# Three ada modulations as TensorE sums, rows spread by step-zero weights, two ga blocks ahead of gb, conv taps back on VectorE

## The chip, the core and the metric

One NeuronCore of a Trainium2 chip. The metric is the device time of one execution in microseconds (us); the kernel before takes 895.0 us (median of three runs, 894.83 to 895.03). Engines are named as in the profile: PE (TensorE), DVE (VectorE), ACT (ScalarE), POOL (GpSimd), SP (the queue that issues all DMAs).

## What is computed

One layer of a diffusion backbone: 512 latent tokens and 256 context tokens of width 1024, all in fp32.

```
mods(6 x 1024) = silu(c) @ w_ada + b_ada          # sh1 sc1 gt1 sh2 sc2 gt2; the same for c_ctx
hl = rmsnorm(x)*(1+sc1)+sh1 ; hc likewise
v, g, xr, gt, ga, gb = split(hl @ w_in)           # xr also of hc
y_a = silu(layernorm(dwconv31(v*sigmoid(g)))) @ w_proj_conv
rec = rglru scans, forward and backward, of dwconv4(xr), started from the context's last state
y_b = (rec * gelu(gt)) @ w_proj_lru
y   = (sigmoid(ga)*y_a + sigmoid(gb)*y_b) @ w_out
x   = x + gt1 * rmsnorm(y)
z   = dwconv3x3((rmsnorm(x)*(1+sc2)+sh2) @ w_up)
x   = x + gt2 * rmsnorm((silu(z_g) * z_v) @ w_down)
```

The six modulations are vectors of 1024. Here m counts them: m = 0, 1 are sh1, sc1 (made early on PE, not touched), m = 2 is gt1, m = 3 is sh2, m = 4 is sc2, m = 5 is gt2.

## The kernel before, in words

Features lie on partitions, tokens in columns. Each fp32 operand of a large product is split into a high part (rounded, on ACT) and a low part (the rest), and `mm3` makes three products, high x high, high x low, low x high. A `block` is eight slices of 128 input features with three products each: 24 products of 512 columns for one block of 128 output features. Weights arrive in the order that the calls of `queue` write down: SP loads a raw tile (three buffers), ACT makes the high part (L122), POOL the low part (L123), or DVE for entries with `eng=V`; `W(key, look)` converts up to `look` entries ahead and asks for DMAs two further. The schedule is manual: each engine runs its instructions in the order of the code, and waits are put in by what tiles an instruction reads and writes.

The order of the work: a start, in which the input is normalised and the first products are made; the LRU loop (L656, rounds b = 1 to 8), in which each round makes xr(b), v(b+1), g(b+2) and the four gate products of b-1 (`gate_mm`), whose results stay in PSUM tiles of 1024 columns (two halves of 512; a gate uses columns 0 to 767); then gt, gb and yb blocks, with ga blocks behind them; the LayerNorm of the conv branch (mean, variance, rstd); the ya blocks; the output projection (y_ps); and the FFN, which takes the last 390 us.

Modulations m = 2 to 5 are summed on DVE: `ada_step(k, w, acc)` multiplies a tile of 128 x 1024 weights with a scalar per partition and adds it to `ggb`, eight steps for a modulation. For m = 2 the steps stand among the context work of the start, for m = 3 two in each of rounds 2 to 5, for m = 4 in the LayerNorm stage, for m = 5 in halves in the FFN. `ada_cols` then sums over partitions by four PE products with ones (four column blocks of 256), copies the result and turns it into columns by two transposes; for m = 2 and 3 that is in rounds 2 and 6. `ada_rows` makes, for m = 2 and 5, a row vector on all partitions: DVE scales the identity by each of eight columns (`dg`), and PE multiplies ones with that, 512 columns at a time (L333). The LayerNorm's rstd row is made the same way (L837, L839).

The depthwise conv of width 31 is a chain of single taps on DVE, handed out by `fill(n)`: n taps at this place in DVE's order. Channel blocks go in pairs. For the last pair (6, 7) the 12 highest taps are not DVE's: `offload(n)` has ACT make the products (L536) and POOL add them (L538), and the pair starts on DVE when all 24 are issued:

```
while n_glu[0] < b0 + 2 or b0 == 6 and off["k"] < 2 * n_off:
    yield False
```

`decay_rates` computes the LRU's decay constants by a chain of small POOL instructions behind one DVE reciprocal (L387). The g2 block's low part is POOL's and stands behind that chain.

Lines to follow: L123 low parts; L303 and L301 `ada_step`; L308, L315 `ada_cols`; L327, L333 `ada_rows`; L512, L504 conv taps; L536, L538 offloaded taps; L554 to L567 the conv of xr; L588 gate tanh; L603 `e` (`r_dve`); L607 `u` (`i_dve`); L809 mean; L830 variance; L839 rstd.

Of the kernel before, what the change touches and what calls it, by code (L numbers as in the profile page):

```python
# [37 lines left out]
def backbone_kernel(es: ExitStack, tc: tile.TileContext, x, ctxt, par, wadq, wada, win, wgate, wpc, wpl, wout,  # L38
# [145 lines left out]
    queue(("g", 2), win[10], wb)  # L184
# [20 lines left out]
    for b in range(NB):  # L205
        queue(("ga", b), win[32 + b], wb)
# [91 lines left out]
    def ada_step(k, w, acc):  # L298
        s = sT[:, k, 0:1]
        if k == 0:  # L300
            V.tensor_scalar(out=acc, in0=w, scalar1=s, scalar2=None, op0=ALU.mult)  # L301
        else:
            V.scalar_tensor_tensor(out=acc, in0=w, scalar=s, in1=acc, op0=ALU.mult, op1=ALU.add)  # L303

    def ada_cols(m, acc, big=None):
        big = cv_tile("ada_cp") if big is None else big
        for j in range(4):
            PE.matmul(big[32 * j:32 * j + 32, 0:256], ones[:, 0:32], acc[:, 256 * j:256 * j + 256], start=True, stop=True)  # L308
        R = t_tile("R2")
        V.tensor_copy(R[:, 0:256], big[:, 0:256])  # L310

        def rest():
# [8 lines left out]

    def ada_rows(m, gain, dst, big=None):
        cl = adl[:, 8 * m:8 * m + 8]
        V.tensor_mul(cl, cl, col(gain))
        dg = [t_tile("dg") for _ in range(2)]
        for n in range(8):
            V.tensor_scalar(out=dg[n // 4][:, 128 * (n % 4):128 * (n % 4) + 128], in0=idn, scalar1=cl[:, n:n + 1],  # L327
                            scalar2=None, op0=ALU.mult)
# [120 lines left out]
    def ctx_h(g, p, i):  # L449
# [19 lines left out]
    ctx_h(0, 0, 3)  # L469
    ctx_h(0, 1, 4)  # L470
# [4 lines left out]
    ctx_h(1, 0, 5)  # L475
    ctx_h(1, 1, 6)
# [50 lines left out]
    n_off = 12  # L527
# [128 lines left out]
    for b in range(1, NB + 1):  # L656
# [31 lines left out]
        fill(0 if last else 2 if b in (2, 6) else 4)  # L688
# [71 lines left out]
    turn[0] = 1  # L760
# [28 lines left out]

# [446 lines left out]
```

## Time and profile before

| | |
|---|---|
| median of 3 runs | 895.0 us (894.83 to 895.03) |
| the profiled execution | 892.42 us, span 890.6 us |
| PE busy | 848.2 us (95%), 4114 products |
| PE weight loads | 686.2 us (77%) |
| DVE busy | 689.3 us (77%), 952 instructions |
| ACT busy | 444.9 us (50%) |
| POOL busy | 441.3 us (50%) |
| chain that ended last | PE 70%, DVE 18%, ACT 5%, issue 4% |

Busy time of PE includes the overlap of pipelined products, so a stage with 100% may still hold a few spare tenths, and a stage below 100% has real gaps. The gaps are found in a timeline: a bracket at a line's end gives the idle time ahead of it and what ended it. PEclk is the clock granted to PE, as a share of full speed.

### The profile page before, as it was taken

The numbers are of one execution on the slowest core, as the hardware profiler recorded it, in microseconds if no ns is written. First come the engines' busy times: TensorE is split into PE (matmuls) and PEld (weight loads), VectorE is DVE, ScalarE is ACT, GpSimd is POOL, SyncE is SP. The second block draws the span as 40 slices with busy tenths as digits, with TensorE's granted clock in tenths as the row PEclk, the third lists the DMA queues.
The fourth block names the chain that finished last, engine by engine and source line by source line (L and its number), as shares of the span: only waits on it lengthen the run. The fifth ranks groups of instructions, "written<-read, shape, count | busy, mean of one in ns | idle before, by whom it ended". The sixth has DMA issues, their size and how long they took to land.

```text
span 890.6 us, 11044 instructions
## 1 busy us (share of the span) xinstructions
PE 848.2 (95%) x4114; PEld 686.2 (77%) x4114; DVE 689.3 (77%) x952; ACT 444.9 (50%) x634; POOL 441.3 (50%) x248
## 2 busy tenths in 40 slices
PE   7997999999999799999897999999999999999997
PEld 6776877877887688887675889988888888888775
DVE  4384799997997999596887345799999898998314
ACT  5282776776667834324833346535434344344322
POOL 1246454554546498946333222446545555547810
PEclk9998999999999999999998999999999999999999
DMA  9943133332123033223534411214333333333502
GB/s 356 384 165 107 60 118 130 107 114 76 60 77 105 33 118 96 95 94 142 193 132 149 166 43 52 93 63 141 118 109 117 118 106 119 107 118 118 166 1 95
DMA packets 31397, 105.98 MB, mean 119 GB/s; under 512 B 3440, under 2 KB 3568, under 8 KB 31344
## 3 DMA queue, kind: packets, MB, share of 16 engines
q1 hardware_dynamic: 31344, 105.29, 34.4%
q8 instruction: 32, 0.52, 0.2%
q14 instruction: 21, 0.17, 0.1%
HBM read 103.17 MB, written 2.10 MB: 118 GB/s over the span
## 4 chain that ended last, share of the span: by engine, by line
PE 70%; DVE 18%; ACT 5%; issue 4%; POOL 2%; DMA 1%; DVEq 0%; SPq 0%; POOLq 0%; ACTq 0%
PE up_ps L135 8%; PE up_ps L136 8%; PE up_ps L134 8%; DVE cv L512 4%; PE xr_ps L134 2%; PE xr_ps L135 2%; PE xr_ps L136 2%; DVE rec L626 2%; DVE ggb L303 2%; PE y_ps L135 2%; PE y_ps L134 2%; PE y_ps L136 2%; PE yb_ps L136 1%; PE yb_ps L135 1%; PE yb_ps L134 1%
## 5 line engine op out<-in xcount | busy, mean ns | idle before, releaser
L123 POOL TENSOR_TENSOR wlo<-raw,whi 128x1024 fp32r<-128x1024 f32 x118 | 293.3, 2498 | 204.2 <-ACT whi L122 203.8
L1034 DVE SCALAR_TENSOR_TENSOR cv<-zall,P,cv 128x512 f32<-128x512 f32 x240 | 161.9, 744 | 0.2
L512 DVE SCALAR_TENSOR_TENSOR cv<-glu,P,cv 128x512 f32<-128x512 f32 x208 | 140.4, 744 | 0.0
L122 ACT ACTIVATE whi<-raw 128x1024 fp32r<-128x1024 f32 x121 | 125.5, 1051 | 21.0 <-issue 8.0
L134 PE MATMUL up_ps<-Ahi,whi 128*128 128x512 f32 (+1 forms) x352 | 131.8, 375 | 0.0
L136 PE MATMUL up_ps<-Ahi,wlo 128*128 128x512 f32 (+1 forms) x352 | 131.7, 374 | 0.0
L135 PE MATMUL up_ps<-Alo,whi 128*128 128x512 f32 (+1 forms) x352 | 131.6, 374 | 0.0
L135 PEld LDWEIGHTS up_ps<-Alo,whi 128*128 128x128 f32 x352 | 66.0, 188 | 13.3
L136 PEld LDWEIGHTS up_ps<-Ahi,wlo 128*128 128x128 f32 x352 | 66.0, 188 | 13.2
L134 PEld LDWEIGHTS up_ps<-Ahi,whi 128*128 128x128 f32 x352 | 66.0, 188 | 13.1
L1020 POOL TENSOR_TENSOR acl<-fo,ach 128x512 fp32r<-128x512 f32 x20 | 26.0, 1301 | 85.5 <-ACT ach L1017 85.5
L1034 DVE SCALAR_TENSOR_TENSOR cv<-zall,P,cc 128x512 f32<-128x512 f32 x40 | 43.2, 1109 | 21.2 <-ACT cc L1008 21.2
L1006 ACT ACTIVATE zall<-up_ps 128x512 f32<-128x512 f32 x40 | 23.8, 594 | 63.5 <-PE up_ps L136 63.5
L588 ACT ACTIVATE gate_ps<-gate_ps,P 128x768 f32<-128x768 f32 x32 | 28.0, 875 | 36.2 <-PE gate_ps L136 35.7
L1017 ACT ACTIVATE ach<-fo 128x512 fp32r<-128x512 f32 x20 | 12.7, 633 | 66.9 <-DVE fo L1016 66.9
L303 DVE SCALAR_TENSOR_TENSOR ggb<-wa,sT,ggb 128x1024 f32<-128x1024 f32 (+1 forms) x35 | 40.1, 1146 | 0.4
L134 PE MATMUL xr_ps<-Ahi,whi 128*128 128x512 f32 x56 | 23.2, 414 | 8.8 <-DVE e L603 8.8
L538 POOL TENSOR_TENSOR off_acc<-off_acc,off_prod 128x512 f32<-128x512 f32 x22 | 28.5, 1318 | 3.9 <-ACT off_prod L536 3.9
L136 PE MATMUL g_ps<-Ahi,wlo 128*128 128x512 f32 x56 | 23.1, 412 | 5.8 <-POOL wlo L123 5.7
L134 PE MATMUL yb_ps<-rgh,whi 128*128 128x512 f32 x64 | 25.8, 404 | 2.5 <-ACT whi L122 2.5
L1008 ACT ACTIVATE cc<-up_ps,P 128x512 f32<-128x512 f32 x40 | 27.3, 682 | 1.9 <-DVE cv L1034 1.9
L136 PE MATMUL yb_ps<-rgh,wlo 128*128 128x512 f32 x64 | 26.0, 406 | 2.2 <-POOL wlo L123 2.2
(386 smaller groups left out, 2156.1 us busy)
## 6 DMA issues: line engine op xcount, KB each, us to landing
raw<-in_win_dram SPq DMA_DIRECT2D x48, 512.0 KB, 3.4
raw<-in_wup_dram SPq DMA_DIRECT2D x40, 512.0 KB, 3.4
wa<-in_wada_dram SPq DMA_DIRECT2D x24, 512.0 KB, 5.6
raw<-in_wdn_dram SPq DMA_DIRECT2D x22, 512.0 KB, 3.4
wa<-in_wadq_dram SPq DMA_DIRECT2D x16, 512.0 KB, 9.2
raw<-in_wpl_dram SPq DMA_DIRECT2D x8, 512.0 KB, 3.3
raw<-in_wpc_dram SPq DMA_DIRECT2D x8, 512.0 KB, 3.6
raw<-in_wout_dram SPq DMA_DIRECT2D x8, 512.0 KB, 3.4
```

Source lines behind the costliest of these rows:

```text
L122: S.activation(out=flat(hl[0]), in_=flat(t), func=AF.Copy)
L123: eng.tensor_sub(flat(hl[1]), flat(t), flat(hl[0]))
L134: PE.matmul(o, lh, rh, start=first, stop=False)
L135: PE.matmul(o, lh, rl, start=False, stop=False)
L136: PE.matmul(o, ll, rh, start=False, stop=last)
L303: V.scalar_tensor_tensor(out=acc, in0=w, scalar=s, in1=acc, op0=ALU.mult, op1=ALU.add)
L512: V.scalar_tensor_tensor(out=cv[b] if k else glu[:, b, 0:T], in0=glu[:, b, k:k + T], scalar=col("dw31", 31 * b + k, 1), in1=cv[b], op0=ALU ...
L538: G.tensor_add(a, a, o)
L588: S.activation(out=lru[b, d, q], in_=lru[b, d, q], func=AF.Tanh, scale=0.5, bias=hb[:, i:i + 1])
L1008: S.activation(out=c, in_=ps.rearrange("p (r c) -> p r c", c=GW), func=AF.Copy, scale=col("dw9", 9 * (i + FW * (1 - s)) + 4, 1))
L1020: G.tensor_sub(acl[:, i, :], fo[i, 0], ach[:, i, :])
L1034: V.scalar_tensor_tensor(out=o, in0=zz[i, s][:, k // 3:k // 3 + GH, k % 3:k % 3 + GW], scalar=col("dw9", 9 * (i + FW * (1 - s)) + k, 1), i ...
```

## The change

- The sums of m = 2, 3 and 4 go to PE. `ada_pe` multiplies `sT[:, k, :]` (32 columns, the first of which is silu(c)) with four column blocks of 256 of the weight tile, and adds up over k in PSUM. m = 2: all eight k at once after the context's xr product. m = 3: two k after the last gate product of rounds 2 to 5, into the free columns 768 to 1023 of that gate's PSUM tile, from which DVE copies or adds them to `ggb`; the turning into columns goes to the end of round 6. m = 4: four k ahead of the variance product, four ahead of ya(0).
- In the loop three taps stand where two steps stood, and rounds 2 and 6 have four taps in place of two at the detour's place.
- `ada_rows` and the LayerNorm's rstd have no diagonal any more: `spread` multiplies, for each of the columns, a weight operand that repeats that column 128 times (step zero) with the identity. The m = 2 rows are issued after ya(3) and no more after ya(5).
- `decay_rates` is issued ahead of the last quarter of hl (`ada_h(3)`); g2's low part goes to DVE.
- ga(0) and ga(1) stand ahead of gb(0) in the queue and in the code.
- The last conv pair has 2 taps on ACT and POOL in place of 12; the first yb round takes 20 taps in place of 8.

```diff
-    queue(("g", 2), win[10], wb)
+    queue(("g", 2), win[10], wb, eng=V)
...
+    for b in (0, 1):
+        queue(("ga", b), win[32 + b], wb)
     queue(("gb", 0), win[40], wb)
...
+    def ada_pe(ks, ws, o, first, last):
+        for n, (k, w) in enumerate(zip(ks, ws)):
+            for j in range(4):
+                PE.matmul(o[32 * j:32 * j + 32, :], sT[:, k, :], w[:, 256 * j:256 * j + 256],
+                          start=first and n == 0, stop=last and n == len(ws) - 1)
...
+    def spread(o, cols, n):
+        for i in range(n):
+            PE.matmul(o[:, 128 * i:128 * i + 128], cols[:, i:i + 1].broadcast_to([128, 128]), idn, start=True, stop=True)
...
     ctx_t(0, 0)
+    decay_rates()
     ada_h(3)
-    for k in range(3):
-        ada_step(k, wa[k], ggb)
-    decay_rates()
...
     block(psA[:, T:T + TP], ready[0], chi, clo)
+    big = cv_tile("ada_cp")
+    ada_pe(range(NB), wa, big[:, 0:256], True, True)
...
+    rest = ada_cols(2, big[:, 0:256], big)
+    w = W(("g", 2), 2, 2)
+    block(psg, w, Ahi, Alo, range(2))
+    rest()
+    block(psg, w, Ahi, Alo, range(2, NB))
...
-    n_off = 12
+    n_off = 2
...
-        if 2 <= b <= 5:
-            for k in (2 * b - 4, 2 * b - 3):
-                ada_step(k, was[k], ggb)
-        else:
-            fill(3)
+        fill(3)
         r_dve(b - 1, 1)
         fill(3)
-        gate_mm(b - 1, 1, 1)
+        ps = gate_mm(b - 1, 1, 1)
+        if 2 <= b <= 5:
+            o = ps[:, TA:1024]
+            ada_pe((2 * b - 4, 2 * b - 3), (was[2 * b - 4], was[2 * b - 3]), o, True, True)
+            if b == 2:
+                V.tensor_copy(ggb[:, 0:256], o)
+            else:
+                V.tensor_add(ggb[:, 0:256], ggb[:, 0:256], o)
+        if b == 6:
+            ada_cols(3, ggb[:, 0:256])(ps[:, T:1024])
         gate_tanh(b - 1, 1, 1)
...
+    turn[0] = 1
+    ga_mm(0)
+    ga_mm(1, look=1)
     gt_act(5)
     gt_act(6)
     gt_act(7)
     gt_post(range(NB))
-    offload(2)
+    offload(4)
...
-        fill(8)
+        fill(8 if b else 20)
...
     def ada4(ks):
+        ada_pe(ks, [was[k] for k in ks], acc4[:, 0:256], ks[0] == 0, ks[-1] == NB - 1)
...
-    dg = t_tile("dg")
-    for t in range(4):
-        V.tensor_scalar(out=dg[:, 128 * t:128 * t + 128], in0=idn, scalar1=rv[:, t:t + 1], scalar2=None, op0=ALU.mult)
-    rl = cv_tile("rstd")
-    PE.matmul(rl, ones, dg, start=True, stop=True)
+    spread(big, rv, 4)
+    rl = big
```

## Rows read from the trace of the kernel before

**Rows 1.** Timeline of PE, gb and yb: start, us, engine, line, operation, count [idle before <-releaser]

```profile
294.45 0.39 PE L134 MATMUL gb_ps<-Ahi,whi 128*128 128x512 f32 x1
...
311.22 0.79 PE L136 MATMUL yb_ps<-rgh,wlo 128*128 128x512 f32 x1 [2.15 <-POOL wlo L123]
...
328.93 0.40 PE L134 MATMUL gb_ps<-Ahi,whi 128*128 128x512 f32 x1
...
334.53 0.39 PE L134 MATMUL yb_ps<-rgh,whi 128*128 128x512 f32 x1
```

**Rows 2.** Timeline of PE at the start.

```profile
71.27 0.80 PE L136 MATMUL g_ps<-Ahi,wlo 128*128 128x512 f32 x1 [5.73 <-POOL wlo L123]
...
78.26 0.39 PE L134 MATMUL xr_ps<-Ahi,whi 128*128 128x512 f32 x1
```

**Rows 3.** Windows, PE alone: us, busy (instructions), PEclk, DMA share, GB/s.

```profile
72.00:76.00 4.00, 4.00 (x13) 0.61 0.72 244
```

**Rows 4.** Timeline of PE in the LRU loop, the first xr product of rounds 3 to 6.

```profile
128.89 0.50 PE L134 MATMUL xr_ps<-Ahi,whi 128*128 128x512 f32 x1 [1.59 <-DVE e L603]
...
155.21 0.50 PE L134 MATMUL xr_ps<-Ahi,whi 128*128 128x512 f32 x1 [2.12 <-DVE e L603]
...
181.53 0.50 PE L134 MATMUL xr_ps<-Ahi,whi 128*128 128x512 f32 x1 [2.12 <-DVE e L603]
...
207.84 0.50 PE L134 MATMUL xr_ps<-Ahi,whi 128*128 128x512 f32 x1 [2.13 <-DVE e L603]
```

**Rows 5.** Windows, all engines: PE, PEld, DVE, ACT, POOL busy, PEclk, DMA share, GB/s.

```profile
208.00:214.00 6.00, 6.00 (x20) 4.74 (x21) 6.00 (x9) 5.94 (x7) 5.49 (x3) 0.72 0.12 44
```

**Rows 6.** Timeline of PE from the mean to the first y_ps.

```profile
410.56 1.02 PE L809 MATMUL mean<-lnsum,ones 128*128 128x512 f32 x2
...
427.55 1.12 PE L839 MATMUL rstd<-dg,ones 128*128 128x512 f32 x2 [2.48 <-DVE dg L837]
...
453.27 0.64 PE L308 MATMUL ada_cp<-ggb,ones 128*32 128x256 f32 x8 [0.80 <-DVE ggb L303]
...
479.64 1.13 PE L333 MATMUL row_ps<-dg,ones 128*128 128x512 f32 x2 [2.99 <-DVE dg L327]
...
482.62 2.04 PE L333 MATMUL row_ps<-dg,ones 128*128 128x512 f32 x2 [1.85 <-DVE gs L901]
...
497.31 0.39 PE L134 MATMUL y_ps<-wo0h,Ahi 128*128 128x512 f32 x1
```

**Rows 7.** Windows, all engines, while rgh and rgl are made.

```profile
306.00:330.00 24.00, 19.50 (x77) 15.42 (x78) 24.00 (x30) 13.96 (x20) 22.17 (x13) 0.93 0.27 88
```

**Rows 8.** Timeline of PE in the first 28 us: products of known size.

```profile
17.94 1.95 PE L340 MATMUL xr_ps<-ones 128*128 128x128 f32 x16
...
25.65 1.95 PE L270 MATMUL ada_ps<-wa,sT 128*32 128x128 f32 x64
```

**Rows 9.** Timeline of POOL behind the decay chain.

```profile
68.85 4.69 POOL L123 TENSOR_TENSOR wlo<-raw,whi 128x1024 fp32r<-128x1024 f32 x2
```

**Rows 10.** Timeline of DVE in round 4 and the steps of its end.

```profile
155.07 2.07 DVE L512 SCALAR_TENSOR_TENSOR cv<-glu,P,cv 128x512 f32<-128x512 f32 x3
...
165.08 1.02 DVE L560 SCALAR_TENSOR_TENSOR xw<-xr_ps,P,xw 128x770 f32<-128x770 f32 x1 [0.59 <-ACT xw L554]
...
177.82 2.80 DVE L303 SCALAR_TENSOR_TENSOR ggb<-wa,sT,ggb 128x1024 f32<-128x1024 f32 x2
```

**Rows 11.** Timeline of ACT in the same round.

```profile
153.13 0.88 ACT L588 ACTIVATE gate_ps<-gate_ps,P 128x768 f32<-128x768 f32 x1 [2.61 <-PE gate_ps L136]
...
164.05 0.99 ACT L554 ACTIVATE xw<-xr_ps,P 128x771 f32<-128x771 f32 x1 [2.50 <-PE xr_ps L136]
```

**Rows 12.** Timeline of DVE in the yb rounds.

```profile
330.75 9.96 DVE L512 SCALAR_TENSOR_TENSOR cv<-glu,P,cv 128x512 f32<-128x512 f32 x15
...
374.01 0.69 DVE L362 SCALAR_TENSOR_TENSOR yb<-tg,yb_ps 128x512 f32<-128x512 f32 x1 [9.20 <-PE yb_ps L136]
...
402.39 1.39 DVE L512 SCALAR_TENSOR_TENSOR glu<-glu,P,cv 128x512 f32<-128x512 f32 x2
```

More of the change, by code (lines that the diff above doesn't have):

```diff
@@ L204, in backbone_kernel @@
         queue(("yb", b), wpl[b], wb)
-    for b in range(NB):
+    for b in range(2, NB):
         queue(("ga", b), win[32 + b], wb)
@@ L295, in ada_h, with ada_cols, rest @@
                     split(h, Ahi[:, k, :], Alo[:, k, :])
[L298 to L301, printed above, removed]
-        else:
[L303 to L312, printed above, removed]
+    def ada_pe(ks, ws, o, first, last):
[3 more added lines that the diff above has]
+                          start=first and n == 0, stop=last and n == len(ws) - 1)
+    def ada_cols(m, src, big=None):
+        if src is None:
+            big = cv_tile("ada_cp") if big is None else big
+            src = big[:, 0:256]
+            for j in range(4):
+                PE.matmul(src[32 * j:32 * j + 32, :], ones[:, 0:32], ggb[:, 256 * j:256 * j + 256], start=True, stop=True)
+        R = src
+        if big is not None:
+            R = t_tile("R2")[:, 0:256]
+            V.tensor_copy(R, src)
+        def rest(big=big):
             tp = big[:, 256:512]
@@ L324, in ada_rows @@
         V.tensor_mul(cl, cl, col(gain))
[L325 to L328, printed above, removed]
         def rest(ns=(0, 1)):
@@ L332, in rest @@
                 ps = cv_tile("row_ps") if big is None else big
-                PE.matmul(ps, ones, dg[n], start=True, stop=True)
+                spread(ps, cl[:, 4 * n:4 * n + 4], 4)
                 S.activation(out=dst[:, 512 * n:512 * n + 512], in_=ps, func=AF.Copy)
@@ L468, in backbone_kernel @@
     ctx_t(0, 1)
-    ctx_h(0, 0, 3)
-    ctx_h(0, 1, 4)
+    ctx_h(0, 0)
+    ctx_h(0, 1)
     firsts((1, 2), (3,))
@@ L687, in backbone_kernel @@
             gt_copy(1 if b < NB else 4)
-        fill(0 if last else 2 if b in (2, 6) else 4)
+        fill(0 if last else 4)
         if not last:
@@ L753, in backbone_kernel, with ga_mm, ga_act @@
     sa = psa.tile([128, NB, T], F32, name="sa")
+    gap = {}
+    def ga_mm(b, ks=range(NB), look=2):
+        if b not in gap:
+            gap[b] = mm_any("ga_ps"), W(("ga", b), look)
+        block(*gap[b], Ahi, Alo, ks)
+    def ga_act(b):
+        S.activation(out=sa[:, b, :], in_=gap[b][0], func=AF.Tanh, scale=0.5)
+    turn[0] = 1
+    ga_mm(0)
+    ga_mm(1, look=1)
     gt_act(5)
@@ L757, in backbone_kernel @@
     gt_post(range(NB))
-    offload(2)
+    offload(4)
     yb = pd.tile([128, NB, T], F32, tag="d", name="yb")
-    turn[0] = 1
+    for b in (0, 1):
+        ga_act(b)
     for b in range(-1, NB):
@@ L777, in backbone_kernel @@
     gs2 = const.tile([128, 8], F32, name="gs2")
-    gap = {}
-    def ga_mm(b, ks=range(NB), look=2):
-        if b not in gap:
-            gap[b] = mm_any("ga_ps"), W(("ga", b), look)
-        block(*gap[b], Ahi, Alo, ks)
-    def ga_act(b):
-        S.activation(out=sa[:, b, :], in_=gap[b][0], func=AF.Tanh, scale=0.5)
     def ada_dma(k):
@@ L794, in ada4 @@
     def ada4(ks):
+        ada_pe(ks, [was[k] for k in ks], acc4[:, 0:256], ks[0] == 0, ks[-1] == NB - 1)
         for k in ks:
-            ada_step(k, was[k], ggb)
             if k < 4:
                 ada_dma(k + 4)
-    for b in range(4):
+    for b in (2, 3):
         ga_mm(b, range(NB if b < 3 else 4))
-        if b:
-            ga_act(b - 1)
         fill(7)
+    ga_act(2)
     fill(1000)
@@ L807, in backbone_kernel @@
         ada_dma(k)
-    mean = cv_tile("mean")
+    mean, acc4 = cv_tile("mean"), cv_tile("ada_cp")
     PE.matmul(mean, ones, lacc[0], start=True, stop=True)
@@ L825, in backbone_kernel @@
     V.tensor_add(sq[:, 0, :], sq[:, 0, :], sq[:, 1, :])
-    ada4(range(0, 2))
     cvt_to(index["ga", 6])
+    ada4(range(4))
     big = cv_tile("var")
@@ L864, in backbone_kernel @@
     ada4(range(4, NB))
+    rest = ada_cols(4, acc4[:, 0:256], acc4)
     for b in (6, 7):
@@ L1060, in ada5 @@
         n = slice(512 * (h % 2), 512 * (h % 2) + 512)
-        ada_step(h // 2, was[5], ggb[:, n])
+        sc = sT[:, h // 2, 0:1]
+        if h < 2:
+            V.tensor_scalar(out=ggb[:, n], in0=was[5], scalar1=sc, scalar2=None, op0=ALU.mult)
+        else:
+            V.scalar_tensor_tensor(out=ggb[:, n], in0=was[5], scalar=sc, in1=ggb[:, n], op0=ALU.mult, op1=ALU.add)
     def ada5_dma(h):
```

26 lines of the change are left out of this document (7 added, 19 removed).

## The prediction

> **What bounds the kernel now.** I read the page's busy shares first, then the table of windows stage by stage, then the TensorE timeline at each stage's seams, then the other engines around each seam. TensorE is the bound nearly everywhere: a block of 24 products takes 5.60 us back to back (334.53 − 328.93) [rows 1], and most stages run at that pace. So the time is the number of blocks, and what TensorE loses between them. The reader is to see four places of loss in the rows. (1) Start: it stands 5.73 us for POOL's low part of g2, then runs 22 products in 6.99 us (71.27 to 78.26) where 5.13 would do; the granted clock there is 0.61 [rows 2, 3]: 1.2 GHz after a stand. (2) Each middle round of the LRU loop: 26.32 us from xr to xr (155.21 to 181.53), with 2.12 us of standing for DVE's e; once the clock falls after it (0.72) [rows 4, 5]. (3) From gb(0) to the mean, 294.45 to 410.56, 116.1 us pass where 19.5 blocks need 109.2 [rows 1, 6]; in 306 to 330 TensorE is busy 19.5 of 24 us while DVE is full [rows 7]. (4) From the mean to the first y_ps, 86.75 us for 12.5 blocks (70.0): stands of 2.48, 0.80, 2.99 and 1.85 us, and after the last one 14.69 us for two blocks (11.2) and half a row product (0.5), so 3.0 to the low clock [rows 6]. DVE is the bound only inside (2) and at the start of (3). All that follows the first y_ps is left as it is but for two row products.
>
> **The change, part by part.** Prices first. A sum of one modulation is 32 products of 256 columns in four column blocks. The old kernel has 32 of 128 columns in 1.95 us (64 records), so I take 3.9 us for the sum, 1.0 for two steps [rows 8]; the four 256-column products of the sum's last step with ones took 0.64 (8 records), which times eight gives 5.1 as the upper end [rows 6], and half of 3.9 is the lower one, should the loads hide better. A spread is four 128-column products; eight such took 1.95 us, so one is 0.98 [rows 8], against about 1 for the 512-column product that it replaces. No row shows a weight load with step zero: taken as an ordinary one, with twice that as the other end.
>
> *Start (m = 2).* Eight DVE steps go (nothing waits for them but POOL's decay chain, queued behind the first three), g2's low part moves from POOL to DVE, which is free by then, and the decay chain starts sooner by those three steps. The 5.73 and the 1.86 of low clock go: −7.6. TensorE gets +3.9 and two transposes (0.25), all of it on the path, since TensorE has no gap left there. xr(1)'s low part is late next: due at about 75, and even at POOL's old time (68.85 plus half of 4.69) it is there at 71.2 [rows 9]. Sum **−3.4** (−2.2 to −5.4).
>
> *LRU loop (m = 3).* In rounds 2 to 5 three taps (2.07) take the place of two steps (2.80) ahead of e on DVE, 0.7 sooner [rows 10]. The two steps' products (1.0) fit in TensorE's 2.12 of standing; their tiles are asked for on SP in the same round, ahead of the g block. But the product lands in columns 768 to 1023 of the gate's own PSUM tile, DVE reads it after three taps, and ScalarE's tanh on columns 512 to 767 of the same half tile is issued behind that read. No row shows two engines on different columns of one half tile. If nothing waits, a round wins 0.7. If tanh waits, it starts not 2.08 us ahead of xr (153.13 against 155.21) but 2.07 + 0.4 behind it (0.4 for the read: a third of the 770-column row), 4.6 later; ScalarE's 2.50 of idle time ahead of xw takes up the rest but 2.1, and xw is on the path, as DVE already waits for it (0.59) [rows 10, 11]. Queued behind tanh on ScalarE are xh, tg, a weight conversion and two square roots; DVE's u and L620, POOL's xl wait for these, and e for all. So −0.7 + 2.1 = +1.4 in rounds 3, 4 and 5. I take the wait, as the nearest row is xr itself, which starts only when the last reader of its tile is done [rows 4].
>
> The Trainium skill, "PSUM — Partial Sum Buffer", section on bank collisions, says that two engines must not touch one bank and quadrant at a time, even on different columns, and that a kernel has to guard them by bank; by it the wait is there and the sum is the one I took, without it 8.2 us less. No run so far shows it.
>
> Round 2 has no such read ahead of it and loses the product with ones and its transposes, and most of its 1.59 [rows 4]: −1.0 (0 to −1.6). Round 6 loses the detour too and has the wait: 0 (−1.9 if the clock holds, +2). The price of a clock fall is 1.7 (0.28 of 6 us) [rows 5]. Sum **+3.2** (−5.0 with no wait; +8.3 with three more clock falls).
>
> *ga ahead of gb, taps back on DVE.* Blocks ga(0) and ga(1) run from 294.45 to 305.7 while DVE makes rgh and rgl, and gb(0), gb(1) after them, so TensorE asks for yb(0) only at about 317, when these are done. The stands and the slow clock in 116.1 go (6.9). What is late next is gb(1)'s low part: it is issued behind ScalarE's four products and POOL's two sums; POOL's low part landed at 311.2 in the old order [rows 1], two sums of some 1.2 (half of a 2.35 low part [rows 9]) put it at 313.6, where TensorE wants it at 311.7: +1.9. Sum **−5.0** (0 to −6.9). DVE gets 20 taps of 0.66 (9.96 for 15) [rows 12], 13.3 us: by the fill counts 16 go into the loop (in the place of steps, or in rounds 2 and 6 where DVE stood anyway), 4 behind it, 2.7 us. The old conv stood 9.20 us since the last pair waited for POOL's sums [rows 12]; with two taps off instead of twelve these are done early. So its end moves from 403.8 to about 397, its sum on POOL some 2.5 later, TensorE comes to the mean at 405.5: covered with 6 us to spare.
>
> *Mean to y_ps (m = 4).* The 8.1 of stands go: DVE's 128-column scalings (diagonals) and its steps, for which TensorE stood, are gone, and the row products come after block 3 with their columns long ready. With them go the 3.0 of low clock. TensorE gets 3.9 and loses 0.64. The first four tiles are asked for behind the ga raws, which POOL, with 20 sums less, frees sooner; they are needed two blocks after the mean. Sum **−7.8** (−4 to −9).
>
> *Tail (m = 5).* Two spreads for two row products on TensorE: **+0.3** (0 to +2).
>
> Sum: −3.4 + 3.2 − 5.0 − 7.8 + 0.3 = −12.7. The profiled execution took 892.42 us (span 890.6 and 1.8 around it), so 879.7; the median shown is 895.0, 2.6 above it, so I forecast 895.0 − 12.7 = **882.3 us**.
>
> **Rivals.** *A: tanh waits for nothing.* The columns are disjoint and DVE's read is short. Then the loop is −5.0: 874.1. *B: the clock falls in the loop.* The widened stands (2.3 in place of 2.12) are as long as the one after which it fell; against it, three of four did not fall. Three more falls: 887.4. *C: the early ga blocks don't fill.* If gb(1) and yb(0) stand for POOL as yb(0) does now, TensorE only stands elsewhere, and that term is 0: 887.3. *D, the other side: conv bounds the mean.* If the last pair still starts at 374 (behind POOL, or as gate products from TensorE pace DVE), the 20 taps lengthen the chain that the old trace ends at 403.8: 417.1, and 2.5 for the sum, so the mean comes at 419.6, 9.0 later, and after such a stand the clock is low (1.9, as at the start): 16 above the forecast, 898.3. It decides from the point where conv's end passes 403 (405.5 less the sum), and costs from there 1 for 1; DVE's full row at 306 to 330 speaks for it [rows 7], the 9.20 of standing against.
>
> **How the numbers follow.** Forecast 0.53 (own range 878 to 886), A 0.22, B 0.11, C 0.08, D 0.06. Low end 873 just takes in A, high end 888.5 B and C; out of the range are D and what the bounds add on either side. About 0.2% (1.8 us) is what a measurement here tells from no change: faster 0.93, same 0.01, slower 0.06.
>
> **What would show it.** Right: no TensorE stand at g2 and full clock to the first gate product; ScalarE's tanh of the fourth gate waits for DVE in rounds 2 to 5 and rounds 3 to 5 last 27 to 28 us; ga at about 290 with one stand of 2 us at gb(1); DVE without the 9.20; no stand at the rows. Wrong: rounds of 25.6 us (A), a granted clock of 0.7 in several rounds (B), TensorE waiting for POOL at yb(0) (C) or at the mean for the sum of conv (D); a sum of 32 products far from 3.9.

## The result and the profile after

The changed kernel takes 883.4 us (median of 4 runs, 882.6 to 884.0) against 895.0 (4 runs, 894.8 to 895.5): a ratio of 0.9869, 95% interval 0.9852 to 0.9886. The forecast was 882.3, range 873.0 to 888.5. The profiled execution of the changed kernel took 883.99 us, with a span of 882.2.

The page after: TensorE is busy for 97% of the span where it was 95%, with 198 products more; DVE and POOL have less to do.

```profile
span 882.2 us, 11379 instructions
...
PE 854.5 (97%) x4312; PEld 691.3 (78%) x4312; DVE 663.0 (75%) x932; ACT 430.7 (49%) x614; POOL 412.7 (47%) x227
```

I divide the span at five first products on TensorE's timeline: the context's xr product of the start, the first gate product, the first ga or gb product behind the loop, the mean, and the first y_ps. Each cell is the difference of two such starts, the last one the span less the start of y_ps. A stand is time in which TensorE waits.

| us | to the context's product | to the first gate | LRU loop | ga, gb, yb to the mean | mean to y_ps | rest |
|---|---|---|---|---|---|---|
| before | 61.99 | 24.81 | 207.65 | 116.11 | 86.75 | 393.3 |
| after | 63.97 | 21.05 | 210.11 | 115.18 | 78.59 | 393.3 |
| difference | +1.98 | −3.76 | +2.46 | −0.93 | −8.16 | 0.0 |
| forecast | 0 | −3.4 | +3.2 | −5.0 | −7.8 | +0.3 |

Most of the first column is not of the change: of the 1.98 us, 1.46 are there already at TensorE's first product of hl (21.79 before, 23.25 after), in code that both kernels share; the clock fell at 12 us in this execution. (Windows, all engines; PEclk is the third number from the end.)

```profile
14.00:16.00 2.00, 2.00 (x22) 1.59 (x22) 0.00 (x0) 0.60 (x1) 0.00 (x0) 0.50 1.03 422
```

The other 0.52 belongs to the change, and the forecast had nothing for it. With the decay chain ahead of the last quarter of hl, DVE waits 0.97 us for the chain's first step on POOL, and TensorE 0.31 us for columns that DVE makes behind it. All thirteen kernels with this order have both waits; from the first product of hl to the context's they take 40.68 us or more, the old one 40.20. DVE and TensorE after:

```profile
51.68 0.25 DVE L393 RECIPROCAL nshalf<-nshalf 128x16 f32<-128x16 f32 x1 [0.97 <-POOL nshalf L389]
```

```profile
55.24 0.63 PE L453 MATMUL tc_ps<-idn,xc_tok 128*128 128x128 f32 x4 [0.31 <-DVE adc L285]
```

The columns add up to −8.4, the spans' difference. The medians differ by 11.6, since the profiled execution of before lay 2.6 us under its median and that of after 0.6 over its own.

*Start.* TensorE's timeline, answering to [rows 2]: no stand at g2 any more; the 32 products of the sum took 3.66 us, and the two transposes come without a wait.

```profile
66.98 3.66 PE L303 MATMUL ada_cp<-wa,sT 128*32 128x256 f32 x64
70.57 0.51 PE L134 MATMUL g_ps<-Ahi,whi 128*128 128x512 f32 x1
72.07 0.38 PE L320 MATMUL ada_cp<-idn,R 128*128 128x128 f32 x2
...
85.02 0.40 PE L134 MATMUL gate_ps<-xh,gwh 128*128 128x512 f32 x1
```

*LRU loop.* TensorE, ScalarE and DVE at the end of a middle round, answering to [rows 4, 10, 11]. Rounds last 27.16 us (153.04 to 180.20) where they lasted 26.32. The sum's two steps take 1.07 us. ScalarE then stands 6.37 us for DVE's read of them (L733), which is queued behind e and three taps; DVE in turn waits 1.02 for the tanh. ScalarE reaches xw 10.62 us behind the first xr product, where it was 8.84 before, and no longer idles ahead of it.

```profile
150.85 1.07 PE L303 MATMUL gate_ps<-wa,sT 128*32 128x256 f32 x16
153.04 0.50 PE L134 MATMUL xr_ps<-Ahi,whi 128*128 128x512 f32 x1 [1.12 <-DVE e L612]
...
180.20 0.50 PE L134 MATMUL xr_ps<-Ahi,whi 128*128 128x512 f32 x1 [1.12 <-DVE e L612]
```

```profile
155.33 0.88 ACT L597 ACTIVATE gate_ps<-gate_ps,P 128x768 f32<-128x768 f32 x1 [6.37 <-DVE ggb L733]
...
163.66 0.98 ACT L562 ACTIVATE xw<-xr_ps,P 128x771 f32<-128x771 f32 x1
```

```profile
152.05 0.94 DVE L612 SCALAR_TENSOR_TENSOR e<-e,gate_ps 128x768 f32<-128x768 f32 x1
152.91 2.06 DVE L520 SCALAR_TENSOR_TENSOR cv<-glu,P,cv 128x512 f32<-128x512 f32 x3
154.89 0.41 DVE L733 TENSOR_TENSOR ggb<-ggb,gate_ps 128x256 f32<-128x256 f32 x1
156.31 0.96 DVE L616 SCALAR_TENSOR_TENSOR u<-gate_ps,xc 128x768 f32<-128x768 f32 x1 [1.02 <-ACT gate_ps L597]
```

*ga, gb, yb.* TensorE's timeline, answering to [rows 1]: the stands at yb(0) are gone, and two others are there, at ga(1) and at gb(1), the second with a low clock behind it (0.72 in the window 314 to 320). 109.2 + 1.58 + 2.55 is 113.3, and the fall accounts for most of what is left of the 115.18.

```profile
295.13 0.39 PE L134 MATMUL ga_ps<-Ahi,whi 128*128 128x512 f32 x1
302.47 0.50 PE L134 MATMUL ga_ps<-Ahi,whi 128*128 128x512 f32 x1 [1.58 <-ACT sa L653]
316.95 0.79 PE L136 MATMUL gb_ps<-Ahi,wlo 128*128 128x512 f32 x1 [2.55 <-POOL wlo L123]
```

Two of the kernels below (diagonals, and m = 4 on DVE) have the same code in this stage and the same two stands, 1.58 or 1.61 and 2.55 us, but the clock holds, and the stage takes 113.82 in both. So the fall costs 1.36 here. TensorE and a window of the first of them:

```profile
317.79 0.50 PE L136 MATMUL gb_ps<-Ahi,wlo 128*128 128x512 f32 x1 [2.55 <-POOL wlo L123]
```

```profile
316.00:322.00 6.00, 4.21 (x18) 3.44 (x19) 6.00 (x7) 0.63 (x1) 6.00 (x3) 1.00 0.36 102
```

What released TensorE from these stands in the changed kernel is read on POOL, DVE and ScalarE. POOL's low part of gb(0) began at 297.71, 0.05 us before DVE's scan (L636), and that scan took 3.97 us; ScalarE's gelu, which frees ga(1)'s PSUM buffer, waits for it. Later POOL's two sums of conv taps (L546) stand ahead of gb(1)'s low part.

```profile
297.71 2.40 POOL L123 TENSOR_TENSOR wlo<-raw,whi 128x1024 fp32r<-128x1024 f32 x1 [0.95 <-ACT whi L122]
...
310.96 3.19 POOL L546 TENSOR_TENSOR off_acc<-off_acc,off_prod 128x512 f32<-128x512 f32 x2 [1.42 <-ACT off_prod L544]
314.10 7.94 POOL L123 TENSOR_TENSOR wlo<-raw,whi 128x1024 fp32r<-128x1024 f32 x3
```

```profile
297.76 3.97 DVE L636 TENSOR_TENSOR_SCAN u<-a,u 128x768 f32<-128x768 f32 x1
```

```profile
301.82 1.58 ACT L653 ACTIVATE sa<-gt_ps 128x512 f32<-128x512 f32 x3 [4.19 <-DVE u L636]
```

DVE has no 9.20 of standing in the yb rounds any more [rows 12]; its last taps end at 398.6, and then it waits 8.49 us for the mean, which comes from TensorE's own order:

```profile
397.19 1.40 DVE L520 SCALAR_TENSOR_TENSOR glu<-glu,P,cv 128x512 f32<-128x512 f32 x2
402.19 0.69 DVE L368 SCALAR_TENSOR_TENSOR yb<-tg,yb_ps 128x512 f32<-128x512 f32 x1 [3.60 <-PE yb_ps L136]
411.37 2.48 DVE L829 SCALAR_TENSOR_TENSOR glu<-mean,glu 128x512 f32<-128x512 f32 x4 [8.49 <-PE mean L822]
```

*Mean to y_ps.* TensorE's timeline, answering to [rows 6]: not one stand of half a microsecond, and full clock. The sum takes twice 1.93 us; the four spread products of the rstd row take 1.05 (L329), the eight of the m = 2 rows 1.95.

```profile
410.31 1.02 PE L822 MATMUL mean<-lnsum,ones 128*128 128x512 f32 x2
...
422.46 1.93 PE L303 MATMUL ada_cp<-wa,sT 128*32 128x256 f32 x32
424.32 1.05 PE L843 MATMUL var<-ones,sq 128*128 128x1 f32 x8
...
426.72 1.05 PE L329 MATMUL var<-idn,rv 128*128 128x128 f32 x8
...
440.30 1.93 PE L303 MATMUL ada_cp<-wa,sT 128*32 128x256 f32 x32
...
464.81 1.95 PE L329 MATMUL row_ps<-idn,adl 128*128 128x128 f32 x16
...
488.90 0.39 PE L134 MATMUL y_ps<-wo0h,Ahi 128*128 128x512 f32 x1
```

### The profile page after: what moved, and what is told of

It reads as the page before. It is cut to its first block, busy times and chain, and to the rows that moved or that the text cites. A ratio compares the mean times of both kernels' runs of the same rounds, so it can differ in the third digit from the quotient of the medians.

```text
span 882.2 us, 11379 instructions
## 1 busy us (share of the span) xinstructions
PE 854.5 (97%) x4312; PEld 691.3 (78%) x4312; DVE 663.0 (75%) x932; ACT 430.7 (49%) x614; POOL 412.7 (47%) x227
## 4 chain that ended last, share of the span: by engine, by line
PE 75%; DVE 11%; ACT 8%; issue 3%; POOL 1%; DMA 0%; DVEq 0%; SPq 0%; ACTq 0%
PE up_ps L135 8%; PE up_ps L134 8%; PE up_ps L136 8%; DVE cv L520 3%; DVE rec L635 3%; PE ya_ps L134 2%; PE y_ps L135 2%; PE yb_ps L136 2%; PE yb_ps L135 2%; PE yb_ps L134 2%; PE ya_ps L136 2%; PE ya_ps L135 2%; PE y_ps L134 2%; PE y_ps L136 2%; PE gb_ps L136 2%
## 5 line engine op out<-in xcount | busy, mean ns | idle before, releaser
L520 DVE SCALAR_TENSOR_TENSOR cv<-glu,P,cv 128x512 f32<-128x512 f32 x228 | 153.8, 745 | 0.0
L1023 ACT ACTIVATE ach<-fo 128x512 fp32r<-128x512 f32 x20 | 12.7, 633 | 66.8 <-DVE fo L1022 66.8
L140 POOL TENSOR_TENSOR xl<-xc,xh 128x768 fp32r<-128x768 f32 x8 | 14.9, 1858 | 45.9 <-ACT xh L139 45.9
L364 ACT ACTIVATE tg<-gb_ps 128x512 f32<-128x512 f32 x8 | 4.8, 596 | 60.2 <-PE gb_ps L136 60.2
L136 PE MATMUL gb_ps<-Ahi,wlo 128*128 128x512 f32 x64 | 26.0, 407 | 2.5 <-POOL wlo L123 2.5
L1040 DVE SCALAR_TENSOR_TENSOR fo<-zall,P,cv 128x512 f32<-128x512 f32 x40 | 27.8, 734 | 0.0
L134 PE MATMUL ga_ps<-Ahi,whi 128*128 128x512 f32 x64 | 26.0, 406 | 1.6 <-ACT sa L653 1.6
```

The costliest lines, as they stand in the source:

```text
L134: PE.matmul(o, lh, rh, start=first, stop=False)
L136: PE.matmul(o, ll, rh, start=False, stop=last)
L520: V.scalar_tensor_tensor(out=cv[b] if k else glu[:, b, 0:T], in0=glu[:, b, k:k + T], scalar=col("dw31", 31 * b + k, 1), in1=cv[b], op0=ALU ...
L1040: V.scalar_tensor_tensor(out=o, in0=zz[i, s][:, k // 3:k // 3 + GH, k % 3:k % 3 + GW], scalar=col("dw9", 9 * (i + FW * (1 - s)) + k, 1), i ...
```

## The experiments

Twelve kernels, all made from the changed one. Stage times are taken as in the table above, each from one profiled execution. Where two kernels differ in one stage, the stage's time is often the sharper measure, as the clock falls at other places from trace to trace, in stages of the same code too. How sharp it is shows in kernels that share a stage's code: the start and the stage from the mean to y_ps agree within 0.02 us, but the loop runs from 209.87 to 211.71 (eight kernels) and the stage of ga, gb and yb from 113.82 to 116.07 (seven).

**The loop: is it the wait?** The theory was the prediction's: the tanh of the fourth gate waits for DVE's read of other columns of its half tile, and that lengthens the rounds. The rival: the extra products and taps do. Three kernels.

*Tanh first*: the tanh is issued ahead of the sum's products.

```diff
...
         ps = gate_mm(b - 1, 1, 1)
+        gate_tanh(b - 1, 1, 1)
         if 2 <= b <= 5:
...
-        gate_tanh(b - 1, 1, 1)
```

> ScalarE's tanh of the fourth gate is issued directly behind the gate's products, ahead of the two steps of the m = 3 sum and of DVE's read of them; all else is as in the changed kernel (883.4 us, rounds 3 to 5 of the LRU loop 27.15 us each). Theory, the wait of the tanh on DVE's read makes these rounds long: the tanh of round 3 starts about 4 us sooner (151.2 in place of 155.33), rounds 3 to 5 fall to about 26, TensorE waits up to 1 us for the tanh ahead of the sum's products in place of 1.12 for e, and the time is 880.0 (878.5 to 881.5). Rival, the rounds are long since TensorE has 16 products more and DVE three taps more, and the tanh waits beside that: rounds stay at 27.1, 883.4 (882.5 to 884.5).

*Read first*: DVE reads the sum ahead of the taps; tanh still behind the read.

```diff
         r_dve(b - 1, 1)
-        fill(3)
+        if not 2 <= b <= 5:
+            fill(3)
         ps = gate_mm(b - 1, 1, 1)
...
                 V.tensor_add(ggb[:, 0:256], ggb[:, 0:256], o)
+            fill(3)
```

> In rounds 2 to 5 DVE reads the two steps of the m = 3 sum directly after e, ahead of the three taps that stood between; ScalarE's tanh is still issued behind that read. Theory, the wait of the tanh on DVE's read makes the rounds long: the tanh starts about 1.9 us sooner (153.4 in place of 155.33 in round 3), what ScalarE has in idle time ahead of xw takes up most of the rest, rounds 3 to 5 fall to about 26.2 and the time is 880.6 (879.3 to 882). Rival, products and taps make the rounds long: 27.1, 883.4 (882.5 to 884.5).

*No sum in the loop*:

```diff
-            ada_pe((2 * b - 4, 2 * b - 3), (was[2 * b - 4], was[2 * b - 3]), o, True, True)
...
-                V.tensor_add(ggb[:, 0:256], ggb[:, 0:256], o)
```

> The m = 3 sum is left out of the loop (its 64 products and DVE's four reads; the accumulator is set to zero once), so this modulation is its bias alone; its weights are still loaded and the turning into columns in round 6 stays. Theory, the wait of the tanh on DVE's read costs the rounds: without product and read there is no wait, and a round of the old loop less the 0.7 us that three taps take less than two steps is 25.6, so the loop wins 4 to 5 us over the changed kernel: 878.8 (877.5 to 880.5). Rival, the three taps in the steps' place make the rounds long: they stay near 27, 883 (881.5 to 884.5).

| | time, us | ratio to before (95%) | loop | a middle round |
|---|---|---|---|---|
| changed kernel | 883.4 | 0.9869 (0.9852 to 0.9886) | 210.11 | 27.16 |
| tanh first | 879.7 | 0.9817 (0.9796 to 0.9839) | 204.64 | 26.17 |
| read first | 875.4 | 0.9777 (0.9757 to 0.9796) | 202.75 | 25.56 |
| no sum | 877.3 | 0.9798 (0.9773 to 0.9822) | 204.30 | 25.57 |

The wait it was. With the read first, the tanh starts 0.31 us behind the first xr product (151.30 against 150.99) instead of 2.29, and TensorE's stand for e shrinks to 0.37. ScalarE and TensorE of that kernel:

```profile
151.30 0.88 ACT L597 ACTIVATE gate_ps<-gate_ps,P 128x768 f32<-128x768 f32 x1 [4.26 <-DVE ggb L734]
```

```profile
150.99 0.50 PE L134 MATMUL xr_ps<-Ahi,whi 128*128 128x512 f32 x1 [0.37 <-DVE e L612]
...
176.55 0.51 PE L134 MATMUL xr_ps<-Ahi,whi 128*128 128x512 f32 x1 [0.38 <-DVE e L612]
```

The expectation had the tanh's 1.9 us right (1.98) and the time 5 us too high: I had let half of the wait vanish in ScalarE's idle time and counted three rounds. 1.60 of the 1.98 came through, in four rounds (3 to 6), and the clock no longer fell at 234 us. Without any sum the time lies 0.2 us under the expected range, and a round is no shorter (its loop is 1.6 longer than with the read first because the clock fell at 281 us): two steps of the sum on TensorE cost nothing when DVE reads them at once. With tanh first the wait changes sides. TensorE's products now wait for the tanh, and a round keeps 0.6 of the loss:

```profile
151.87 1.07 PE L303 MATMUL gate_ps<-wa,sT 128*32 128x256 f32 x16 [0.97 <-ACT gate_ps L597]
```

The Trainium skill, "PSUM — Partial Sum Buffer", section "PSUM bank collisions raise a hardware error", has software keep two engines apart on one bank even on different columns; the schedule's waits here agree with it in both orders (6.37 and 0.97 us), while no run shows what the bank does without them.

**The start: what does the sum cost?**

*m = 2 on DVE*: the eight `ada_step`s go back to their old places, the decay chain and g2's low part stay as in the changed kernel.

```diff
-    ada_pe(range(NB), wa, big[:, 0:256], True, True)
...
+    for k in range(3):
+        ada_step(k, wa[k], ggb)
...
-    rest = ada_cols(2, big[:, 0:256], big)
...
+    rest = ada_cols(2, None)
```

> The m = 2 sum goes back to DVE (eight steps at their old places, summed over partitions by four products with ones behind the g2 block), while the decay chain stays ahead of the last quarter of hl and g2's low part stays on DVE. Theory, the 32 products cost TensorE their whole 3.66 us and the gain of the start came from g2's low part alone: TensorE loses 3.66 us, gains 0.64 for the products with ones, and DVE, which stood 10 us in this stretch, takes eight steps of 1.4 us: 880.7 (879.5 to 882). Rival, DVE's steps push the low parts of the context or of g2 behind TensorE's need, and the stand at g2 or at the context's product comes back: 883.5 to 887.

880.0 us (ratio 0.9826, 0.9802 to 0.9850). From the context's product to the first gate 18.01 us pass where the changed kernel has 21.05. TensorE goes from the context's products to g2 and xr without a stand:

```profile
71.21 0.64 PE L318 MATMUL ada_cp<-ggb,ones 128*32 128x256 f32 x8
71.78 0.50 PE L134 MATMUL xr_ps<-Ahi,whi 128*128 128x512 f32 x1
```

So the start's gain is that of g2's low part on DVE and the decay chain's earlier place (−6.8, 24.81 to 18.01), and the sum on TensorE gives 3.0 of it back: 3.66 less 0.64. No run separates the two. By the rows it is g2's low part: here POOL's chain ended at 67.4, only 1.4 us sooner than the old one's 68.8, and no stand followed. What the chain's earlier place shows by itself is its cost of 0.5 us ahead of the context's product.

**ga ahead of gb: where did the 5 us go?** Four kernels.

*ga behind*: ga(0) and ga(1) back behind yb, in queue and code.

```diff
-    for b in (0, 1):
-        queue(("ga", b), win[32 + b], wb)
...
-    ga_mm(0)
-    ga_mm(1, look=1)
```

> ga(0) and ga(1) go back behind the yb blocks, in the order of weights and in the code; two taps offloaded and all else as in the changed kernel (883.4 us). Theory, the two early blocks only move TensorE's stands (from yb(0) to ga(1) and gb(1)) and win about the 0.9 us by which gb(0) to mean got shorter: 884.3 (883 to 886). Rival, the early blocks are worth the 5.0 us of the forecast, and what was lost comes from fewer taps on ScalarE and POOL: 888.4 (886.5 to 890).

888.9 us (ratio 0.9923, 0.9904 to 0.9941), the stage 120.17. This lies in the rival's range, and read alone it would say that the early blocks are worth the 5.0 of the forecast. The rows say something else. POOL's low part of one rgl block took 7.00 us where the old trace has 1.59 for the same instruction, and yb(0)'s low part, behind it and two sums, was late by 5.85. POOL and TensorE of this kernel:

```profile
301.71 7.00 POOL L140 TENSOR_TENSOR rgl<-ge,rgh 128x512 fp32r<-128x512 f32 x1 [6.03 <-ACT rgh L139]
308.67 1.26 POOL L140 TENSOR_TENSOR rgl<-sa,rgh 128x512 fp32r<-128x512 f32 x1
309.90 2.49 POOL L544 TENSOR_TENSOR off_acc<-off_acc,off_prod 128x512 f32<-128x512 f32 x2
```

```profile
314.75 0.80 PE L136 MATMUL yb_ps<-rgh,wlo 128*128 128x512 f32 x1 [5.85 <-POOL wlo L123]
```

*ga behind, two taps ahead*: the same with `offload(2)` in place of `offload(4)` ahead of the yb rounds, as the old kernel had it.

```diff
-    offload(4)
+    offload(2)
```

> As the kernel with ga(0) and ga(1) back behind yb (888.95 us; 120.2 us from gb(0) to the mean, where the old kernel had 116.1), but with only two offloaded products ahead of the yb rounds, as the old kernel had. Theory, what made that stage 4 us longer than the old one is POOL's two sums (2.5 us) ahead of yb(0)'s low part, and a low part of rgl that took POOL 7.00 us where the old trace has 1.59, which started 0.4 us sooner against DVE: without the sums yb(0)'s low part comes 2.5 us sooner, 886.4 (884.5 to 887.5), and if POOL's 7.00 goes too, 884 (883 to 885). Rival, the stage is longer for another reason (fewer taps on ScalarE and POOL): 889 (888 to 890.5).

886.2 us (ratio 0.9893, 0.9876 to 0.9911). POOL's block takes 1.59 again, the stage is 115.05:

```profile
303.42 1.59 POOL L140 TENSOR_TENSOR rgl<-ge,rgh 128x512 fp32r<-128x512 f32 x1 [6.04 <-ACT rgh L139]
```

Against the changed kernel's 115.18 the two early blocks are thus worth next to nothing in their stage as they were built, with one fall of the clock in either (at 314 us here, at 316 there); where the clock holds, the changed kernel's stage is 1.2 shorter than this one. The stands mostly moved. The median, though, is 2.2 above the 884 expected for the case that POOL's 7.00 goes too, and all five executions (885.7 to 886.7) lie above the four of the changed kernel. (The 2.2 us by which this profiled execution is longer than that of the changed kernel lie in the start, 0.6, and in the loop, 1.6, where the clock fell at 290 us. One trace can't tell whether that fall belongs to the edit, so up to 2.7 us of the median stay open.)

*Twelve taps offloaded again*:

```diff
-    n_off = 2
+    n_off = 12
```

> The last conv pair has 12 taps on ScalarE and POOL again in place of 2; all else as in the changed kernel (883.4 us). Theory, the taps are off the path either way: the pair starts on DVE at about 370 and ends, with 38 taps of 0.66 us, at about 396, its sums on POOL by 404, ahead of the 410.3 at which TensorE comes to the mean; POOL has 20 sums of 1.6 us beside 16 low parts of 2.4 in 90 us: 883.8 (882.5 to 885.5). Rival, POOL's sums push the low parts of gb and yb behind TensorE's need, or the end of conv behind the mean: 887 to 895.

883.0 us (ratio 0.9862, 0.9840 to 0.9884), the stage 114.97: the theory. DVE stands 10.51 us shortly ahead of the last pair, and its last taps end at 406, still ahead of the mean at 409. The taps are off the path either way: the last sums of conv end on POOL at 408.0 with twelve offloaded, at 400.5 with two.

*POOL's order mended*: gb(0)'s conversion behind one gelu, the offloaded taps behind the conversions of gb(1) and yb(0).

```diff
-    ga_mm(0)
-    ga_mm(1, look=1)
+    ga_mm(0, look=1)
+    ga_mm(1, look=0)
     gt_act(5)
+    cvt_to(index["gb", 0])
...
-    offload(4)
...
             t = tn
+            offload(4)
             continue
```

> Of the changed kernel (883.4 us) only two things are issued later: gb(0)'s conversion behind the gelu of block 5, and the four offloaded products with their sums behind gb(1)'s and yb(0)'s conversions. Theory, the 5.0 us of the forecast for the early ga blocks were lost to POOL's order: POOL's low part of gb(0) beside DVE's long scan (3.97 us in place of 1.73) made gelu, and with it ga(1)'s buffer, late (1.58), and its sums stood ahead of gb(1)'s low part (2.55, and 1.7 of low clock behind it): the scan takes 1.7 us again, both stands go, 877.9 (876.5 to 880). Rival, TensorE then comes to yb(0) ahead of the last low parts of rgl and stands there: 882 to 884.

879.6 us (ratio 0.9819, 0.9799 to 0.9840). The stage takes 109.59 us, the 109.2 of its 19.5 blocks, and both stands are gone. Two things were moved together here; that each answers to one stand is read from what the stands had waited for. TensorE, then DVE's scan, in this kernel:

```profile
296.41 0.40 PE L134 MATMUL ga_ps<-Ahi,whi 128*128 128x512 f32 x1
307.61 0.40 PE L134 MATMUL gb_ps<-Ahi,whi 128*128 128x512 f32 x1
318.81 0.39 PE L134 MATMUL yb_ps<-rgh,whi 128*128 128x512 f32 x1
```

```profile
297.50 1.72 DVE L636 TENSOR_TENSOR_SCAN u<-a,u 128x768 f32<-128x768 f32 x1
```

The stage won 5.6; the time won 3.9, since the clock fell once more in the loop (at 289 us, after the stand of 1.5 that the changed kernel has there too, without a fall).

**Mean to y_ps: spreads or sum?**

*Diagonals*: rows and rstd by DVE's scalings and a product with ones again, at the new places.

```diff
-                spread(ps, cl[:, 4 * n:4 * n + 4], 4)
+                PE.matmul(ps, ones, dg[n], start=True, stop=True)
...
-    spread(big, rv, 4)
+    PE.matmul(rl, ones, dg, start=True, stop=True)
```

> The row vectors (m = 2, m = 5 and the LayerNorm's rstd) come from diagonals made on DVE and a product with ones again, at the places that the spreads have in the changed kernel (883.4 us); all sums stay on TensorE. Theory, of the 8.2 us from the mean to the first y_ps the spreads brought what TensorE stood for the rstd diagonal, 2.48, while the stands at the m = 2 rows went with their earlier place: TensorE stands 2.5 us at the rstd row again, nothing at the m = 2 rows, 885.9 (885 to 887.5). Rival, the step-zero loads bring the stage's whole gain: 890 to 892.

883.9 us (ratio 0.9867, 0.9848 to 0.9887), the stage 78.79: both theory and rival wrong. Nothing stands for the diagonals. DVE's four scalings take 0.88 us here; in the old trace they took 2.96 (before, then this kernel):

```profile
424.54 2.96 DVE L837 TENSOR_SCALAR dg<-idn,rv 128x128 f32<-128x128 f32 x4
```

```profile
425.31 0.88 DVE L854 TENSOR_SCALAR dg<-idn,rv 128x128 f32<-128x128 f32 x4
```

In the old trace POOL's low part of a weight (424.80, 2.42 us) ran beside them; here that low part comes later (426.10).

*m = 4 on DVE*, spreads kept:

```diff
-        ada_pe(ks, [was[k] for k in ks], acc4[:, 0:256], ks[0] == 0, ks[-1] == NB - 1)
         for k in ks:
+            ada_step(k, was[k], ggb)
...
+        if b == 1:
+            rest = ada_cols(4, None)
```

> The m = 4 sum goes back to DVE (two steps ahead of the variance, two behind the rstd row, four behind the LayerNorm), with the four products with ones behind ya(1) and the m = 2 rows ahead of ya(5)'s end; the spreads stay. Theory, the sum on TensorE costs its 3.86 us and brought nothing by itself, since the stands were those of the diagonals: TensorE loses 3.86, gains 0.64 and a stand of about 0.8 at the products with ones: 881.0 (879.5 to 882.5). Rival, DVE's steps delay the LayerNorm's low parts and the first ya block or the columns for the rows: 884 to 888.

882.2 us (ratio 0.9848, 0.9824 to 0.9871), the stage 76.48, 2.1 less than with the sum on TensorE: the theory, with a stand of 0.96 at the products with ones where 0.8 was expected. The median shows only 1.2 of it, from executions of 879.1 to 883.6, and its interval overlaps that of the changed kernel; the reading rests on the stage.

```profile
447.84 0.64 PE L318 MATMUL ada_cp<-ggb,ones 128*32 128x256 f32 x8 [0.96 <-DVE ggb L311]
```

So either cure was enough: with the sum off DVE the diagonals cost 0.2, and with the diagonals gone (and the columns for the rows made a block earlier than before) the sum on DVE costs nothing but that stand. No run has both the sum on DVE and the diagonals at the new places, so what the earlier place of the rows is worth by itself is not shown.

**Together.** *Four edits*: read first, m = 2 on DVE, and both parts of POOL's order.

> Four edits of the changed kernel together: DVE reads the m = 3 steps ahead of the taps (875.4 us alone), the m = 2 sum on DVE (3.0 us less to the first gate product), and gb(0)'s conversion and the offloaded taps later. Theory, the edits lie in three stages and add: 875.4 - 3.0 - 5.5 = 866.9 (865 to 869.5). Rival, the edits in the gb stage win nothing as TensorE then waits at yb(0): 872.4 (871 to 873.5).

870.9 us (ratio 0.9719, 0.9697 to 0.9741). The stages are 18.01, 202.99, 110.84 and 78.59: they add nearly as expected, but TensorE waits 0.99 for POOL at gb(1) again. The profiled execution took 869.1, inside the expected range; the median is 1.8 above it and outside, just short of the rival's 871.

*Seven edits*: also m = 4 on DVE, and two of order:

```diff
-        fill(3)
+        if not last:
+            fill(3)
         r_dve(b - 1, 1)
-        fill(3)
+        if not 2 <= b <= 5:
+            fill(6 if last else 3)
...
+    cvt_to(index["gb", 1])
     for b in (0, 1):
         ga_act(b)
```

> The four edits that took 870.87 us together, and three more: the m = 4 sum on DVE with the spreads kept (2.1 us less from the mean to the first y_ps, in the trace of that edit alone), DVE's e ahead of the taps in the loop's last round (TensorE stood 1.52 for it ahead of the last gt block), and gb(1)'s conversion ahead of ScalarE's tanh of the two ga blocks (TensorE stood 0.99 for its low part). Theory, a stage in which TensorE is the bound wins what TensorE no longer waits or computes, and the terms add: 870.9 - 4.6 = 866.3 (864.5 to 868). Rival, DVE or POOL takes over as the bound of one of these stages: 869 to 871.

868.0 us (ratio 0.9690, 0.9677 to 0.9703), the fastest: 15.4 less than the changed kernel and 27.8 less than before in the same comparison. The stages are 18.01, 201.21, 112.29 and 76.45. The median is at the upper end of the expected range: against the four edits the loop is 1.78 shorter and the ga, gb, yb stage 1.45 longer. What the last round won came back for the most part at ga(1), whose buffer the gelu frees no sooner (it starts 207.4 us behind the first gate product in both), and gb(1) still waits. So nearly all of the gain over the four edits is m = 4 on DVE, 2.1. TensorE of this kernel:

```profile
290.34 0.50 PE L134 MATMUL ga_ps<-Ahi,whi 128*128 128x512 f32 x1 [1.13 <-ACT sa L662]
...
303.07 0.50 PE L136 MATMUL gb_ps<-Ahi,wlo 128*128 128x512 f32 x1 [0.79 <-POOL wlo L123]
```

## Why the prediction was right, and where not

- *Start* (−3.4, measured −3.76): the parts of this stage as put. The decay chain's earlier place, counted as free, cost 0.52 in the stretch before it, so the change's own gain is 3.2. The sum took 3.66 for an estimated 3.9, scaled by columns from the 128-column row.
- *LRU loop* (+3.2, measured +2.46): the mechanism was the one forecast, shown by the two kernels that undo the wait. The tanh starts 2.3 us behind xr, where 2.5 was worked out. A middle round lost 0.84 instead of 1.4: xw started 1.78 later where 2.1 was worked out, and DVE no longer waited for ScalarE ahead of e behind it (0.32 before). Round 2 won 1.22 for 1.0, round 6 won 0.37 for 0, and the rounds from 7 on lost 1.54, for which the sum had nothing, as the clock fell in round 7; in the old trace it fell in round 6. Rival A, in which tanh waits for nothing, is out, and its sum for the loop, −5.0, is what the read-first kernel has (202.75 against 207.65).
- *ga ahead of gb* (−5.0, measured −0.93): the step that failed, within its range. In this stage rival C, in which TensorE only stands elsewhere, is what came nearly true, with the stands at ga(1) and gb(1) and not at yb(0). "What is late next is gb(1)'s low part" was right in place and nearly in size (2.55 for 1.9). Missing were two things: the clock falls after that stand, as it did after the stands that were removed, so the low clock of the old stage was not wholly gone (1.36, and not at all in two kernels in which the clock held); and two more weights in the queue put gb(0)'s low part beside DVE's scan, which cost ga(1) 1.58. With these mended the stage is what the blocks need. The sign "ga at about 290" did not follow from the prediction's own sums, which give 294.3 (294.45 − 3.4 + 3.2); ga came at 295.1.
- *Taps back on DVE*: covered, as forecast; rival D is out, as conv's last sum ends on POOL at 400.5, 9.8 us ahead of the mean, for the 6 forecast. They also bring nothing that shows: with twelve offloaded the stage is the same within 0.2, far less than it varies from kernel to kernel.
- *Mean to y_ps* (−7.8, measured −8.16): the sum is right, its division was not. I gave the gain to steps and diagonals together and charged TensorE 3.9 for it; the runs show that with the spreads the steps could have stayed on DVE, 2.1 cheaper. A weight operand with step zero costs what an ordinary one was put at (1.05 and 1.95 us for 0.98 and 1.95); the doubled price did not come.
- *Tail* (+0.3, measured 0): eight spread products beside the rest of that stage cost nothing that shows.
- *The base*: the four stages that moved add to −10.4, not −12.7, as the 4.1 missing between ga and the mean were made up only in part by the start, the loop, the mean stage and the tail (0.4, 0.7, 0.4 and 0.3). With the +1.98 of the first column the two profiled executions differ by 8.4. That the forecast is yet within 1.1 of the measured median is luck: the profiled execution of before lay 2.6 under its median and that of after 0.6 over its own, which adds 3.2 to the difference of the medians.

## What to carry to other kernels

Moving a vector sum to TensorE pays only where TensorE has standing time to give: here it was free in the loop and cost its full 3.0 and 2.1 us in two stages in which TensorE is the bound. When a product lands in the free columns of a tile that another engine works on, put its reader first: three taps of order were worth 8 us, 1.0 of it a fall of the clock that did not come; the whole change won 11.6. And count stands in a stage by what POOL and DVE have queued there, for a block moved into a gap brings its weight conversion along.

## What the runs showed that I had not expected

POOL and DVE hold each other up by whole instructions. DVE's scan took 3.97 us where POOL's 2.40 us low part had begun 0.05 us before it, against 1.72 alone. In two other kernels (tanh first, twelve taps) the low part began 0.03 and 0.02 us ahead of the scan, and there it was POOL that took 3.97 and 3.96 us and the scan 1.73; ga(1) then had no stand, and gb(1) stood 1.15 for ScalarE and 2.76 and 2.74 for POOL. Which of the two is held up thus turned on hundredths of a us. POOL with twelve taps, beside a scan that began at 296.89:

```profile
296.87 3.96 POOL L123 TENSOR_TENSOR wlo<-raw,whi 128x1024 fp32r<-128x1024 f32 x1 [0.98 <-ACT whi L122]
```

POOL's 512-column low part took 7.00 where it takes 1.59 in two other kernels, although it came up at the same point of DVE's run of two-input products in all three (2.66 us behind its start, not sooner, as I had put it in the expectation); DVE's products kept their pace meanwhile (three in 1.89 us, against 3.00 in the old trace, where POOL got through), and POOL's instruction ended 1.2 us behind the last of them, when DVE had gone over to taps (307.48). The Trainium skill, "SBUF — State Buffer", section "SBUF: two separate sides", has a port pair that the two engines lock for a whole instruction, also for DVE instructions with two SBUF inputs; the scan agrees to a tenth (2.35 of waiting and 1.72 make 4.07), the 7.00 are more than one DVE instruction long, so by that rule POOL would have lost the pair to one after another until the run was over. Why it did there and not elsewhere stays open.

The clock falls to 1.2 GHz after some stands and not after others of the same length: after 1.5 us at 289 us in one kernel and not in another, after 2.55 us at gb(1) in the changed kernel and not in two others, and in some executions at 12 or 22 us in code that all of them share (the context products of the thirteen kernels start between 62.6 and 64.9 us). A fall costs 1.0 us net (from round 7 to ga(0): 60.62 us in the changed kernel, 59.62 with the read first) to 1.6 (the loop without the sum), and 1.36 between ga and the mean. What decides it stays open, and it sets how small an effect a median here can tell.
